# A decoder trunk of two layers: the low parts of the MLP weights of groups 1 to 7 made on VectorE from a second rounded copy that ScalarE writes into two PSUM banks

## The chip, the cores and the metric

The kernel runs on one core of a Trainium2 chip. The metric is the device time of one execution in microseconds (us). The kernel before takes 1218.79 us, the median of three runs (1218.43 to 1220.8).

## The reference

The trunk has two layers on 512 tokens of width 1024. The first mixes tokens by attention, the second by a short convolution; each is followed by an MLP of width 4096 with a squared ReLU and by a gated input embedding. All arithmetic is in float32. The part that matters here:

```python
def sq_relu_mlp(h, w_up, w_down):
    return jnp.square(jax.nn.relu(h @ w_up)) @ w_down
...
        f = sq_relu_mlp(rmsnorm(x, g[2]), w_mlp_up[i], w_mlp_down[i])
        x = x + rmsnorm(f, g[3])
        gate = jax.nn.sigmoid(rmsnorm(x, g[4]) @ w_ple_gate[i])
        e = (p[i] @ w_ple_proj[i]) * gate
        x = x + rmsnorm(e, g[5])
```

## The kernel before, in words

**High and low parts.** Every matrix product runs as three products of rounded operands (`mm3`, L268 to L270): high by high, low by high and high by low, added up in one PSUM bank. An operand x is split (`split`, L274): ScalarE writes the high part `hi`, which is x rounded to the type fp32r (L276), and another engine writes the low part, x less `hi` (L277). For a weight these tiles are called `wh` and `wl`. The other engine is VectorE, except for a few forms for which `prepare` (L175) names GpSimd: the weight sums T1 to T4 of the MLP's groups 1 to 6, and the sums S3 and S4 of the convolution's projections.

**Weights.** A fixed list (`plan` and what calls it) holds all weight tiles of 128x512 in the order of their use. SyncE's queue loads them as `raw` tiles. `prepare` walks the list some eight tiles ahead of the matmuls; for each tile it loads, and splits.

**The MLP** (`mlp`, L957) has eight groups of 512 hidden units, `gr` 0 to 7, in each layer. Groups 0 to 6 run like this:

- *Up.* For four blocks f of 128 hidden units, 8 x 3 matmuls of 128x512 fill a bank `up_<gr>_<f>`. ScalarE applies ReLU (tile `r`, L975) and squares (tile `q`, L961). Group 0 runs in two halves of 256 tokens (`r_0_2_256` is the second half of block 2); the others run whole. That is 96 matmuls of 128x512.
- The squares are cut into quarters A11 to A22, and GpSimd makes sums S1 to S4 of them (L989). Each is split into high and low parts (`A12h`, `S1h`, `S3l`); two of them share a tile.
- *Down* (`down`). The product of 2x2 blocks is done with seven products rather than eight, in the order 1, 2, 4, 5, 6, 7, 3. The weight blocks are B11 to B22 (`raw`) and the sums T1 to T4 (`dn_T`), which GpSimd makes at L168. Each product fills two banks (`dn_<gr>_50` and `dn_<gr>_51` for product 5) by 2 x 2 x 3 matmuls: 84 in all.
- The seven products are gathered in 14 accumulator tiles `acc` in SBUF. In group 0, ScalarE copies the banks there (L1018); from group 1 on, VectorE adds the bank to the tile (L1021). In group 1, these additions are also ordered behind the low part of S3 and S4 by a dependence written by hand.

Group 7 runs up like the others, and down as a plain product with eight weight tiles. Then the norm, the residual and the gated embedding follow, token tile by token tile.

**PSUM.** All eight banks come from one pool (`bank`, L83). A tile takes the bank that came free first and waits for its last reader. The names above without their numbers are those of the profile: `dn`, `up`, `acc`.

**Order.** A scheduler sets the order of the instructions on each engine when the kernel is built, so a change in `split` can move other instructions too. Each engine works through its own queue in order.

Of the kernel before, what the change touches and what calls it, by code (L numbers as in the profile page):

```python
# [9 lines left out]
F32R = mybir.dt.float32r  # L10
AF = mybir.ActivationFunctionType
ALU = mybir.AluOpType
# [42 lines left out]
ON_POOL = ('S3', 'S4')  # L55
# [13 lines left out]
def trunk(ctx: ExitStack, tc, x, xT, pT, g, gT, wv, wqk, bf, wo, wci, wcq, cw, wco, wup, wdn, wpp, wpg, out):  # L69
    nc = tc.nc  # L70
# [9 lines left out]
    def page(name, dtype=F32):  # L80
        return pages.tile([P, S], dtype, tag="pg", name=name)

    def bank(name):  # L83
        return psum.tile([P, S], F32, tag="ps", name=name)
# [67 lines left out]
    def fetch(upto):  # L152
        while len(fetched) < min(upto, len(loads)):
            n = len(fetched)
            raw = raws.tile([P, S], F32, tag="raw", name=f"raw{n}")
            fetched.append(raw)
            src = loads[n]
            nc.sync.dma_start(raw[:, : src.shape[-1]], src)

    def derive(key):  # L160
        at, sums = recipes.pop(key)
        fetch(max(at.values()) + 1)
        B = {name: fetched[n][:, :S] for name, n in at.items()}
        for name, a, b, op in sums:
            t = page("_".join(str(u) for u in (*key, *name)))
            derived[(*key, *name)] = t
            B[name] = t[:, :S]
            ins = nc.gpsimd.tensor_tensor(out=B[name], in0=B[a], in1=B[b], op=op)  # L168
            if last_norm:
                tc.add_manual_dep(  # L170
                    ins.ins, last_norm.pop().ins.name,
                    mybir.DependencyInfo(mybir.DependencyClass.Sync, mybir.DependencyReason.DATA),
                )

    def prepare(upto, lows=None):  # L175
        while begun[0] < min(upto, len(order)):
            n = begun[0]
            begun[0] += 1
            key, at = order[n]
            for of in (key[:3], key[:2]):  # L180
                if of in recipes:
                    derive(of)
            hi, lo = page(f"wh{n}", F32R), page(f"wl{n}", F32R)
            if isinstance(at, tuple):
                raw, w = derived.pop(key), S
                eng = nc.gpsimd if (key[0] == "dn" and key[2] > 0) or key[-1] in ON_POOL else nc.vector
            else:
                fetch(at + 1)
                raw, eng, w = fetched[at], lows or nc.vector, loads[at].shape[-1]
                fetched[at] = None  # L190
            if key[0] in ("v", "qk"):
                split_gained(hi, lo, raw, w, key[2], eng, key[0] == "qk" or key[1] == 2)
            else:
                split(hi[:, :w], lo[:, :w], raw[:, :w], eng)
            ready[key] = Pair(hi[:, :w], lo[:, :w])

    def wide(*key, soon=SOON):

        prepare(where[key] + 1 + soon)
        return ready[key]  # L200
# [73 lines left out]
    def split(hi, lo, src, eng=nc.vector):  # L274

        nc.scalar.copy(hi, src)  # L276
        return eng.tensor_tensor(out=lo, in0=src, in1=hi.bitcast(F32), op=ALU.subtract)  # L277

    def split_gained(hi, lo, src, w, at, eng, paired):

        parts = [(slice(0, w), at)]
        if paired:
            parts = [(slice(256 * i, 256 * i + 256), 2 * at + i) for i in range(2)]
        for c, k in parts:
            nc.scalar.mul(hi[:, c], src[:, c], first_g[:, k : k + 1])
        for c, k in parts:
            eng.scalar_tensor_tensor(
                out=lo[:, c], in0=src[:, c], scalar=first_g[:, k : k + 1],
                in1=hi[:, c].bitcast(F32), op0=ALU.mult, op1=ALU.subtract,
            )  # L290
# [49 lines left out]
    def keep(t, n, ps, hT):  # L340
        to = lambda h: h[:, 4 * n : 4 * n + 4, t * P : (t + 1) * P]
        split(to(hT.hi), to(hT.lo), ps.rearrange("p (j c) -> p j c", j=4))
# [51 lines left out]
    def mixer_out(kind, lhs, xs, gB, then, opened):  # L394


        mgs, sums = {}, {}
        for t, n in BLOCKS:
            if (t, n) == (2, 0):
                prepare(where[kind, 1, KT - 1] + 1 + SOON)  # L400
            at = (t, n) in opened
            ps = opened.pop((t, n)) if at else bank(f"{kind}{n}_{t}")
            for k in range(KT - 1 if at else 0, KT):
                mm3(ps, lhs(k, t), wide(kind, n, k, soon=soon(t, n)), k == 0, k == KT - 1)
            sums[t, n] = squares(ps, f"{kind}s{n}_{t}")
            mgs[t, n] = gained(ps, gB, n, f"{kind}m{n}_{t}")
            if (t, 1 - n) in mgs:
                residual(t, *([d.pop((t, i)) for i in range(2)] for d in (mgs, sums)), xs[t],
                         f"{kind}r")
                then(t)  # L410

    def attention(hT, raw_x, b_f, warm, work, by_hand):
# [6 lines left out]
        def logs():  # L419

            e, u, lg = stat("f_e", n_f), stat("f_u", n_f), stat("f_l", n_f)
            neg = stat("f_n", n_f)
            nc.vector.tensor_scalar(out=neg, in0=logit, scalar1=-1.0, scalar2=None, op0=ALU.mult)
            nc.vector.tensor_tensor(out=neg, in0=logit, in1=neg, op=ALU.min)
            nc.scalar.activation(e, neg, AF.Exp)
            yield
            nc.vector.tensor_scalar(out=u, in0=e, scalar1=1.0, scalar2=None, op0=ALU.add)
            nc.scalar.activation(lg, u, AF.Ln)
            rest, ru = stat("f_r", n_f), stat("f_ru", n_f)
            nc.vector.scalar_tensor_tensor(  # L430
                out=rest, in0=u, scalar=-1.0, in1=e, op0=ALU.add, op1=ALU.subtract
            )
            nc.vector.reciprocal(ru, u)
            nc.vector.tensor_tensor(out=rest, in0=rest, in1=ru, op=ALU.mult)
            yield
            nc.vector.tensor_tensor(out=lg, in0=lg, in1=rest, op=ALU.subtract)
            logf = stat("logf", n_f)
            nc.vector.scalar_tensor_tensor(
                out=logf, in0=logit, scalar=0.0, in1=lg, op0=ALU.min, op1=ALU.subtract
            )  # L440
            split(lf.hi, lf.lo, logf)
            yield
# [235 lines left out]
        def stream():  # L678
            for i in range(1, KT):
                for n, _ in enumerate(project(i)):  # L680
                    yield
                    if i == KT - 1 and n > KT:
                        streaming.clear()
                        reach[0] = (n - KT - 1) // 2
                        split_o()
            yield from out_part((0,), range(6))
            yield from out_part((1,), range(6))
            prepare(where["o", 1, KT - 1] + 1)
            yield from out_part((0, 1), (6,))
# [630 lines left out]
```

## Time and profile before

| | |
|---|---|
| median of 3 runs | 1218.79 us (1218.43 to 1220.8) |
| the profiled execution: span | 1216.5 us |
| the profiled execution: what lies around its span, taken as median less span | 2.3 us |
| mean clock granted to TensorE | 0.999 |
| TensorE (PE) | 1205.5 us busy, 6175 instructions |
| VectorE (DVE) | 931.4 us busy, 1474 instructions |
| ScalarE (ACT) | 691.4 us busy, 1465 instructions |
| GpSimd (POOL) | 655.4 us busy, 616 instructions |
| moved by DMA | 150.84 MB, mean 124 GB/s |

The profile is of one execution. Its rows name the engine, the line (L276 is line 276 of the kernel before), the operation, and the tiles as out<-in, without their numbers. A row of a time line holds the start, the duration (from the first start to the last end, if several are gathered, with their number behind x), and in brackets the idle time ahead of it with what ended it. Matmuls overlap: a row of 0.39 us may start 0.23 us behind the one ahead of it, so times are read from start to start. Casts of ScalarE overlap too, by about a tenth of a microsecond.

### The profile page before, as it was taken

Reading aid. Unit: us, or ns where it says so; the run is one execution under the profiler, and the core shown is the slowest. Engines: PE = TensorE matmul, PEld = TensorE weight load, DVE = VectorE, ACT = ScalarE, POOL = GpSimd, SP = SyncE. Lnnn points to the kernel's source line nnn. Section 1 sums busy time; section 2 is a strip of 40 time slices with the busy share of each in tenths; the row PEclk is TensorE's granted clock in tenths of the full one; section 3 lists DMA queues with packets and bytes.
Section 4 is the critical chain, followed back from the end, with each engine's and each line's share of the span. In section 5 each row is a group of like instructions: output and inputs, shape, how many; then the busy total and the mean of one; then the engine's idle time right before and its main releaser. Section 6 shows DMA issues by size and latency. Waiting matters only on the chain.

```text
span 1216.5 us, 18743 instructions
## 1 busy us (share of the span) xinstructions
PE 1205.5 (99%) x6175; PEld 1027.5 (84%) x6175; DVE 931.4 (77%) x1474; ACT 691.4 (57%) x1465; POOL 655.4 (54%) x616
## 2 busy tenths in 40 slices
PE   9999999999999999999999999999999999999997
PEld 8888887898888888888889999989888888888886
DVE  7888889586669766879877888866876787669873
ACT  7687778458644564455665534545746445645551
POOL 2035666155787877774213455126676878678210
PEclk9999999999999999999999999999999999999999
DMA  9376544623234323438223123542422443135401
GB/s 333 122 210 172 167 152 125 222 93 94 77 113 138 102 66 110 139 97 276 83 88 108 35 80 103 176 154 71 139 87 65 127 138 106 61 112 185 162 13 58
DMA packets 87314, 150.84 MB, mean 124 GB/s; under 512 B 10352, under 2 KB 18080, under 8 KB 87216
## 3 DMA queue, kind: packets, MB, share of 16 engines
q1 hardware_dynamic: 86640, 149.11, 39.3%
q8 instruction: 49, 0.80, 0.3%
q10 hardware_dynamic: 576, 0.53, 0.1%
q14 instruction: 49, 0.40, 0.1%
HBM read 139.03 MB, written 6.37 MB: 120 GB/s over the span
## 4 chain that ended last, share of the span: by engine, by line
PE 91%; ACT 3%; issue 2%; DVE 2%; POOL 1%; DMA 0%; SPq 0%; POOLq 0%; DVEq 0%; ACTq 0%
PE up L269 9%; PE up L270 9%; PE up L268 9%; PE dn L268 8%; PE dn L270 8%; PE dn L269 8%; PE v L476 3%; PE pg L269 2%; PE pg L268 2%; PE pg L270 2%; PE qk L270 2%; PE qk L269 2%; PE qk L268 2%; PE pT L590 1%; PE co L269 1%
## 5 line engine op out<-in xcount | busy, mean ns | idle before, releaser
L277 DVE TENSOR_TENSOR wl<-raw,wh 128x512 fp32r<-128x512 f32 x346 | 344.7, 1041 | 14.1 <-ACT wh L276 13.4
L269 PE MATMUL up<-hTh,wl 128*128 128x512 f32 (+1 forms) x576 | 210.2, 365 | 0.0
L270 PE MATMUL up<-hTl,wh 128*128 128x512 f32 (+1 forms) x576 | 209.6, 365 | 0.0
L268 PE MATMUL up<-hTh,wh 128*128 128x512 f32 (+1 forms) x576 | 208.7, 366 | 0.0
L276 ACT CAST wh<-raw 128x512 fp32r<-128x512 f32 x346 | 189.4, 625 | 4.5 <-DVE xd L373 4.4
L975 ACT ACTIVATE r<-up 128x512 f32<-128x512 f32 (+1 forms) x72 | 39.5, 548 | 201.8 <-PE up L270 190.1
L277 POOL TENSOR_TENSOR wl<-dn_T,wh 128x512 fp32r<-128x512 f32 x96 | 132.7, 1416 | 30.0 <-ACT wh L276 30.0
L168 POOL TENSOR_TENSOR dn_T<-raw,raw 128x512 f32<-128x512 f32 x56 | 87.0, 1564 | 69.1 <-DMA raw<-in_wdn 50.5
L269 PEld LDWEIGHTS up<-hTh,wl 128*128 128x128 f32 x576 | 108.6, 189 | 17.5
L268 PEld LDWEIGHTS up<-hTh,wh 128*128 128x128 f32 x576 | 108.6, 189 | 17.5
L270 PEld LDWEIGHTS up<-hTl,wh 128*128 128x128 f32 x576 | 108.2, 189 | 17.4
L1021 DVE TENSOR_TENSOR acc<-dn,acc 128x512 f32<-128x512 f32 x168 | 107.4, 680 | 13.9 <-PE dn L270 13.9
L168 POOL TENSOR_TENSOR dn_T<-raw,dn_T 128x512 f32<-128x512 f32 x56 | 92.5, 1651 | 2.2
L276 ACT CAST wh<-dn_T 128x512 fp32r<-128x512 f32 x112 | 61.4, 616 | 10.9 <-POOL dn_T L168 10.9
L277 DVE TENSOR_TENSOR A12l<-q,A12h 128x512 fp32r<-128x512 f32 x28 | 23.2, 829 | 53.8 <-ACT A12h L276 53.8
L1035 POOL TENSOR_TENSOR acc<-acc,acc 128x512 f32<-128x512 f32 x28 | 46.9, 1707 | 9.9 <-DVE acc L1021 9.9
L277 DVE TENSOR_TENSOR A11l<-q,A11h 128x256 fp32r<-128x256 f32 x28 | 23.2, 828 | 36.5 <-ACT A11h L276 36.5
L270 PE MATMUL qk<-hTl,wh 128*128 128x512 f32 x128 | 50.7, 396 | 0.0
L269 PE MATMUL pg<-wh,hTl 128*128 128x512 f32 x128 | 50.5, 394 | 0.0
L268 PE MATMUL pg<-wh,hTh 128*128 128x512 f32 x128 | 50.4, 394 | 0.0
L268 PE MATMUL qk<-hTh,wh 128*128 128x512 f32 x128 | 50.3, 393 | 0.0
L269 PE MATMUL qk<-hTh,wl 128*128 128x512 f32 x128 | 50.2, 392 | 0.0
(404 smaller groups left out, 3304.5 us busy)
## 6 DMA issues: line engine op xcount, KB each, us to landing
raw<-in_wup SPq DMA_DIRECT2D x128, 256.0 KB, 2.9
raw<-in_wdn SPq DMA_DIRECT2D x128, 256.0 KB, 2.8
raw<-in_wcq SPq DMA_DIRECT2D x36, 256.0 KB, 2.8
raw<-in_wqk SPq DMA_DIRECT2D x32, 256.0 KB, 5.3
raw<-in_wpg SPq DMA_DIRECT2D x32, 256.0 KB, 4.1
g<-in_g SPq DMA_DIRECT2D x22, 256.0 KB, 5.9
prl<-neg_c SPq DMA_DIRECT2D x16, 256.0 KB, 6.3
raw<-in_wo SPq DMA_DIRECT2D x16, 256.0 KB, 4.7
```

The source lines that it names most:

```text
L168: ins = nc.gpsimd.tensor_tensor(out=B[name], in0=B[a], in1=B[b], op=op)
L268: nc.tensor.matmul(ps, a.hi, b.hi, start=start, stop=False)
L269: nc.tensor.matmul(ps, a.lo, b.hi, start=False, stop=False)
L270: nc.tensor.matmul(ps, a.hi, b.lo, start=False, stop=stop)
L276: nc.scalar.copy(hi, src)
L277: return eng.tensor_tensor(out=lo, in0=src, in1=hi.bitcast(F32), op=ALU.subtract)
L476: nc.tensor.matmul(ps[:, : V_CHUNKS[c][1]], getattr(of_x(k, t), p), getattr(ready["v", c, k], of), start=k == 0 and p == of, stop=k == KT ...
L590: nc.tensor.transpose(ps[:, b * P : (b + 1) * P], probs[h][b][:, j * P : (j + 1) * P], ident)
L975: nc.scalar.activation(r[:, :n], ps[:, :n], AF.Relu)
L1021: ins = nc.vector.tensor_tensor(out=a, in0=banks[s], in1=a, op=ALU.add)
L1035: nc.gpsimd.tensor_tensor(out=a, in0=a, in1=acc[i, s][:, :S], op=ALU.add)
```

## The change

For the weights of the MLP's groups 1 to 7, up and down, `prepare` now calls a new function, `split_beside`. ScalarE rounds each weight twice: once into `hi`, as before, and once into a bank of PSUM. VectorE makes the low part from the source and the copy in PSUM, not from `hi`; the value is the same. There are two such banks for each layer, `beside_0` and `beside_1`. They are used in turn, are taken from the pool at the first use (which falls in group 0, since weights are prepared ahead), and are held until the last weight of group 7. Matmuls have six banks meanwhile. GpSimd makes no low part of T1 to T4 any more. In numbers, for both layers: 2 x (56 + 84 + 8) = 296 more casts on ScalarE; 96 low parts go from GpSimd to VectorE; loads and matmuls are the same.

```diff
             if isinstance(at, tuple):
                 raw, w = derived.pop(key), S
-                eng = nc.gpsimd if (key[0] == "dn" and key[2] > 0) or key[-1] in ON_POOL else nc.vector
+                eng = nc.gpsimd if key[-1] in ON_POOL else nc.vector
...
             if key[0] in ("v", "qk"):
                 split_gained(hi, lo, raw, w, key[2], eng, key[0] == "qk" or key[1] == 2)
+            elif key[0] in ("up", "dn") and key[2] > (key[0] == "up"):
+                split_beside(hi[:, :w], lo[:, :w], raw[:, :w], key[1])
             else:
                 split(hi[:, :w], lo[:, :w], raw[:, :w], eng)
...
+    besides = {}
+
+    def split_beside(hi, lo, src, l):
+
+        n = besides[l, "n"] = 1 - besides.get((l, "n"), 1)
+        if (l, n) not in besides:
+            besides[l, n] = bank(f"beside{l}_{n}")
+        again = besides[l, n][:, : src.shape[-1]]
+        nc.scalar.copy(again.bitcast(F32R), src)
+        nc.scalar.copy(hi, src)
+        nc.vector.tensor_tensor(out=lo, in0=src, in1=again, op=ALU.subtract)
```

(The third number of an "up" key counts half groups, so the condition holds from group 1 on for both.)

The two places at which the new order matters most lie in the down step of group 0. The first is on ScalarE, from the last half block of up to the accumulator copies. Before (line, operation, out<-in; L975 is ReLU, L961 the square, L276 a cast to a high part, L1018 a copy of a bank to an accumulator):

```order
L975 ACTIVATE r_0_2_256_4063<-up_0_2_256_4038 128x256
L961 ACTIVATE q_0_2_3750<-r_0_2_256_4063 128x256
L975 ACTIVATE r_0_3_256_4093<-up_0_3_256_4068 128x256
L961 ACTIVATE q_0_3_3751<-r_0_3_256_4093 128x256
L276 CAST A12h_0_3_4096<-q_0_3_3751 128x512
...
L1018 COPY acc_1_0_4134<-dn_0_10_4112 128x512
L1018 COPY acc_1_1_4136<-dn_0_11_4113 128x512
L276 CAST wh_4140<-dn_0_T_0_3771 128x512
L276 CAST wh_4150<-dn_0_T_1_3779 128x512
L1018 COPY acc_2_0_4160<-dn_0_20_4138 128x512
L1018 COPY acc_2_1_4162<-dn_0_21_4139 128x512
```

And of the changed kernel, whose lines lie up to 14 lower in the file:

```order
L989 ACTIVATE r_0_2_256_4063<-up_0_2_256_4038 128x256
L975 ACTIVATE q_0_2_3750<-r_0_2_256_4063 128x256
L289 CAST beside_0_4196<-raw_4194 128x512
L989 ACTIVATE r_0_3_256_4093<-up_0_3_256_4068 128x256
L975 ACTIVATE q_0_3_3751<-r_0_3_256_4093 128x256
...
L1032 COPY acc_1_0_4134<-dn_0_10_4112 128x512
L1032 COPY acc_1_1_4136<-dn_0_11_4113 128x512
L278 CAST wh_4140<-dn_0_T_0_3771 128x512
L289 CAST beside_1_4210<-raw_4208 128x512
L278 CAST wh_4150<-dn_0_T_1_3779 128x512
L1032 COPY acc_2_0_4160<-dn_0_20_4138 128x512
L1032 COPY acc_2_1_4162<-dn_0_21_4139 128x512
```

The first two weights of group 1 get their copies here: one cast moves in ahead of the last ReLU of group 0, and one between the casts of two weights of product 6 and 7, ahead of the copies of product 2. Layer 1 has the same order.

The second place is on TensorE, in the same step (product 5, around the second half of products 2 and 4). Before:

```order
L268 MATMUL dn_0_50_4190<-wh_3881,S1h_0_1_4030 128x512
L269 MATMUL dn_0_50_4190<-wh_3881,S1l_0_1_4031 128x512
L270 MATMUL dn_0_50_4190<-wl_3882,S1h_0_1_4030 128x512
L268 MATMUL dn_0_51_4191<-wh_3881,S1h_0_1_4030 128x512
L269 MATMUL dn_0_51_4191<-wh_3881,S1l_0_1_4031 128x512
L270 MATMUL dn_0_51_4191<-wl_3882,S1h_0_1_4030 128x512
L268 MATMUL dn_0_20_4138<-wh_3815,A12h_0_3_4096 128x512
...
L268 MATMUL dn_0_50_4190<-wh_3891,S1h_0_3_4104 128x512
L268 MATMUL dn_0_51_4191<-wh_3891,S1h_0_3_4104 128x512
```

And of the changed kernel:

```order
L270 MATMUL dn_0_50_4190<-wh_3881,S1h_0_1_4030 128x512
L271 MATMUL dn_0_50_4190<-wh_3881,S1l_0_1_4031 128x512
L272 MATMUL dn_0_50_4190<-wl_3882,S1h_0_1_4030 128x512
L270 MATMUL dn_0_20_4138<-wh_3815,A12h_0_3_4096 128x512
...
L272 MATMUL dn_0_50_4190<-wl_3892,S1h_0_3_4104 128x512
L270 MATMUL dn_0_51_4191<-wh_3881,S1h_0_1_4030 128x512
L271 MATMUL dn_0_51_4191<-wh_3881,S1l_0_1_4031 128x512
L272 MATMUL dn_0_51_4191<-wl_3882,S1h_0_1_4030 128x512
L270 MATMUL dn_0_51_4191<-wh_3891,S1h_0_3_4104 128x512
```

The second bank of product 5 is filled as a whole behind the first. With two banks fewer, other tiles share banks: `dn_0_50` takes the bank that the last ReLU (`r_0_3_256`) empties, before that of `r_0_2_256`; `dn_0_51` that which the first copy of product 1 empties (`acc_1_0`); and `dn_0_60`, product 6, that of `dn_0_20`, which `acc_2_0` empties, where before it took that of `dn_0_10`, which `acc_1_0` empties.

## The prediction

> **What bounds the kernel now.** I read the page first, then the chain of waits, the windows and the time lines of single engines around the MLP. The page's busy times and the chain's engine line (share of the span by engine):
>
> ```profile
> PE 1205.5 (99%) x6175; PEld 1027.5 (84%) x6175; DVE 931.4 (77%) x1474; ACT 691.4 (57%) x1465; POOL 655.4 (54%) x616
> PE 91%; ACT 3%; issue 2%; DVE 2%; POOL 1%; DMA 0%; SPq 0%; POOLq 0%; DVEq 0%; ACTq 0%
> ```
>
> TensorE bounds the kernel, and only some 11 us of the 1216.5 are not its own. Rows of the chain that start two groups in the MLP of each layer (start, duration, engine, tile, line), and the window of one group (columns: PE, PEld, DVE, ACT, POOL busy, then clock, DMA share, GB/s):
>
> ```profile
> 322.03 0.45 PE dn L268 x2
> 362.83 0.45 PE dn L268 x2
> 932.80 0.91 PE dn L268 x4
> 973.60 0.91 PE dn L268 x4
> ...
> 363.00:404.00 41.00, 41.00 (x183) 33.96 (x182) 31.82 (x37) 20.55 (x38) 31.15 (x24) 1.00 0.32 103
> ```
>
> Both pairs lie exactly 40.80 us apart. A group has 96 + 84 = 180 matmuls, so each takes 0.2267 us and nothing is lost between them. In groups 1 to 6 the low parts are hidden, whoever makes them. A gain for VectorE or GpSimd there has no stall to remove; ScalarE, 20.55 us of 41, has room. What can change the time is a place where the new casts or the two missing banks reach TensorE. The tightest is the down step of group 0, where ScalarE empties the banks. TensorE's rows there (layer 0):
>
> ```profile
> 280.59 0.39 PE L270 MATMUL dn<-wl,A12h 128*128 128x512 f32 x1
> 280.89 0.50 PE L268 MATMUL dn<-wh,S1h 128*128 128x512 f32 x1
> ...
> 282.18 0.40 PE L270 MATMUL dn<-wl,S1h 128*128 128x512 f32 x1
> 282.71 1.20 PE L268 MATMUL dn<-wh,A12h 128*128 128x512 f32 x4
> 283.75 0.39 PE L269 MATMUL dn<-wh,A12l 128*128 128x512 f32 x1
> ...
> 286.71 0.39 PE L270 MATMUL dn<-wl,S1h 128*128 128x512 f32 x1
> 287.03 0.50 PE L268 MATMUL dn<-wh,S1h 128*128 128x512 f32 x1
> ```
>
> The last row is product 6 (dn_0_60). ScalarE's rows of the same time:
>
> ```profile
> 281.19 0.37 ACT L975 ACTIVATE r<-up 128x256 f32<-128x256 f32 x1
> ...
> 282.04 0.62 ACT L276 CAST A12h<-q 128x512 fp32r<-128x512 f32 x1
> ...
> 285.36 1.14 ACT L276 CAST wh<-dn_T 128x512 fp32r<-128x512 f32 x2
> 286.40 1.06 ACT L1018 COPY acc<-dn 128x512 f32<-128x512 f32 x2
> 287.36 1.15 ACT L276 CAST wh<-dn_T 128x512 fp32r<-128x512 f32 x2
> 288.40 1.08 ACT L1018 COPY acc<-dn 128x512 f32<-128x512 f32 x2
> ```
>
> From 285.36 ScalarE never pauses: two casts of weights, two copies of accumulators, and again. Product 6 starts at 287.03, right behind the first copy of 286.40 (x2 in 1.06 us, the first done near 286.98): TensorE already waits on ScalarE here for a bank.
>
> **The change, part by part.** First the prices: casts of ScalarE in one unbroken row, the same cast by itself and at half width, the two kinds of low part, the accumulator's addition (which reads a bank of PSUM), and a low part while GpSimd is idle (groups: total busy us, mean ns of one, then the idle time before them):
>
> ```profile
> 364.81 7.39 ACT L276 CAST wh<-raw 128x512 fp32r<-128x512 f32 x14
> ...
> L276 ACT CAST wh<-raw 128x512 fp32r<-128x512 f32 x346 | 189.4, 625 | 4.5 <-DVE xd L373 4.4
> L276 ACT CAST A11h<-q 128x256 fp32r<-128x256 f32 x28 | 11.4, 407 | 0.9
> ...
> L277 DVE TENSOR_TENSOR wl<-raw,wh 128x512 fp32r<-128x512 f32 x346 | 344.7, 1041 | 14.1 <-ACT wh L276 13.4
> L277 POOL TENSOR_TENSOR wl<-dn_T,wh 128x512 fp32r<-128x512 f32 x96 | 132.7, 1416 | 30.0 <-ACT wh L276 30.0
> L1021 DVE TENSOR_TENSOR acc<-dn,acc 128x512 f32<-128x512 f32 x168 | 107.4, 680 | 13.9 <-PE dn L270 13.9
> 393.48 0.69 DVE L277 TENSOR_TENSOR S1l<-s,S1h 128x512 fp32r<-128x512 f32 x1 [2.10 <-ACT S1h L276]
> ```
>
> *One more cast, b.* Fourteen casts in 7.39 us are one every 0.52 us (7.39 less the last one's 0.62, by 13). No row shows ScalarE writing to PSUM. From below I bound b by the half-width cast's 0.41 less the 0.09 by which neighbours overlap (0.62 - 0.52): 0.32; from above by the lone cast's 0.625. I take 0.52, since these casts stand in a queue and have the same shape. The Trainium skill (ScalarE: Activation LUTs, section "Step-by-step: what each stage is for") says that ScalarE writes to PSUM faster than to SBUF, but that this only pays where TensorE doesn't need most of PSUM. By its first half b would lie below 0.52, and with the lower bound the sum below is 5.3 instead of 6.1 us; its second half speaks against this change, and the waits for a bank at 287.03 agree with it.
>
> *A low part on VectorE.* 1.04 us now, mean; 0.69 undisturbed; 0.68 for the addition with a bank as one operand, while GpSimd works. I take 0.68 for the new form, as the nearest row. A group has 8 + 14 = 22 of these low parts, 14 on VectorE and 8 on GpSimd before. VectorE: 31.82 - 14 x 1.04 + 22 x 0.68 = 32.2 us of 40.8 (at 1.04 it would be 40.1). GpSimd: 31.15 - 8 x 1.42 = 19.8. ScalarE: 20.55 + 22 x 0.52 = 32.0. All fit, so groups 2 to 6 cost and gain nothing: the cover is 40.8 us of matmuls, the fullest engine under it 32.2. The Trainium skill (Advanced Engine Details and Errata, section "GPSIMD Details") has GpSimd share a read and a write interface with VectorE, with conflicts where VectorE reads two operands of SBUF. The rows (1.04 with two, 0.68 with a bank) agree; without this rule VectorE would stand at 40.1 of 40.8, a rival below.
>
> *Group 0's down step.* The order of the changed kernel puts the first cast into a bank between q_0_2 and the last relu (281.19), the second between the two weight casts of 287.36. Both stand ahead of accumulator copy 2. And with two banks gone, product 6 no longer takes the bank of product 1 but that of product 2; it waits for the copy of 288.40 rather than that of 286.40. So:
> - the copy comes 288.40 - 286.40 = 2.00 us later in the queue;
> - two casts ahead of it: 2 x 0.52 = 1.04 us;
> - product 6 at 287.03 + 3.04 = 290.07.
>
> On the way TensorE stands in pieces that add up to this, not on top of it: product 5's first bank now waits for the relu (done at 281.56 before, 282.08 now, against 280.89); A12h comes 0.52 later; product 5's second bank waits for acc 1's copy (287.5). TensorE is bound and wins none of it back: from there on its next banks (products 7, 3, group 1's up) are copied 0.6 us or more ahead of it. The low parts and weights aren't late, as the raw weight of the first cast landed long before. Layer 1 has the same order:
>
> ```profile
> 854.98 0.50 PE L268 MATMUL dn<-wh,S1h 128*128 128x512 f32 x1
> 854.36 1.06 ACT L1018 COPY acc<-dn 128x512 f32<-128x512 f32 x2
> 856.35 1.08 ACT L1018 COPY acc<-dn 128x512 f32<-128x512 f32 x2
> ```
>
> There 856.35 - 854.36 + 1.04 = 3.03 us.
>
> *Group 1.* Between accumulator copy 2 and S3h of group 1's last pair ScalarE gets 16 more casts, with the two before them 18 x 0.52 = 9.4 us. Its pauses there (in brackets):
>
> ```profile
> 303.03 0.60 ACT L975 ACTIVATE r<-up 128x512 f32<-128x512 f32 x1 [1.40 <-PE up L270]
> 306.43 0.60 ACT L975 ACTIVATE r<-up 128x512 f32<-128x512 f32 x1 [1.70 <-PE up L270]
> 311.33 0.62 ACT L276 CAST S1h<-s 128x512 fp32r<-128x512 f32 x1 [2.98 <-POOL s L989]
> ...
> 317.31 0.60 ACT L975 ACTIVATE r<-up 128x512 f32<-128x512 f32 x1 [0.86 <-PE up L270]
> ...
> 321.17 0.62 ACT L276 CAST S1h<-s 128x512 fp32r<-128x512 f32 x1 [1.95 <-POOL s L989]
> ```
>
> They hold 8.9 us, and TensorE itself comes 3 us later, so this just fits. But VectorE's accumulator additions of group 1 stand behind S3's low part by a dependence written by hand, and banks wait for them. I take 0 and keep 1 us a layer (two casts) for the range.
>
> *Group 7, and what follows the MLP*: the same casts in place of none, eight weights that lie ready early; taken at nothing, the cover being the group's 96 + 192 matmuls.
>
> The sum: 3.04 + 3.03 = 6.07, or 6.1 us. The profiled execution goes from 1216.5 to 1222.6 us of span. The median stands 2.3 us above the span (1218.79 against 1216.5: what lies around it), so the time is 1218.8 + 6.1 = **1224.9 us**, 0.5% slower. A measurement here can tell 0.2%, 2.4 us, from no change.
>
> **The rivals.**
> *A, the forecast*: chance 0.80.
> *B, ScalarE becomes the bound in every group.* Its pauses for GpSimd's sums stay, in a group:
>
> ```profile
> 392.83 0.62 ACT L276 CAST S1h<-s 128x512 fp32r<-128x512 f32 x1 [2.88 <-POOL s L989]
> ...
> 402.67 0.62 ACT L276 CAST S1h<-s 128x512 fp32r<-128x512 f32 x1 [1.84 <-POOL s L989]
> ```
>
> With these 4.7 us its group is 20.55 + 4.7 + 22b; it passes 40.8 at b = 0.71. At 0.8, 42.9: 2.1 us x 12 groups = 25 us, and group 0's 2 x 3.6 = 7.2: 1251 us. For it: no row shows the cast. Against: every cast in the trace is below 0.63, and GpSimd, relieved, ends those pauses earlier. Chance 0.06.
> *C, no change, by relief.* VectorE's low parts drop to 0.68, and TensorE's waits in the MLP go: in the rows above 0.07 us before 280.89, 0.30 before 282.71, 0.13 before 283.75, 0.09 before 287.03, 0.6 a layer, 1.2 in all: 1217.6. It decides if product 6 doesn't wait for copy 2, if ScalarE, say, ran its queue with 3 us to spare there. Against: it shows no pause from 285.36 on, and a start of TensorE right behind a copy. Chance 0.09.
> *D, VectorE becomes the bound.* The low part stays at 1.04: 40.1 us, and the pause of 2.10 at 393.48 makes 42.2: 1.4 x 12 = 17 us, with the 6.1 of group 0 1242 us. Against: 168 additions at 0.68. Chance 0.05.
>
> **How the numbers follow.** Low end: b = 0.32 gives 2 x (2.00 + 0.64) = 5.3; less 1.2 of relief, less the 0.4 by which the fastest run lies under the median: 1222.5. High end: b = 0.625 gives 6.5, two stalls of 1 us in group 1, and the 2.0 us by which the slowest run lies above the median: 1229.3. B, C and D, 0.20 together, stay outside. Slower: A, B, D less a little of A's low end, 0.89. Same: C, 0.09 with that little. Faster, for which no row has 2.4 us to give: 0.02.
>
> **What would show it.** In the profile of the changed kernel: product 6 of group 0 near 290.1 in layer 0, with TensorE's pauses before it on ScalarE's relu, A12h and copies; the starts of groups from there on 40.80 us apart; ScalarE's casts into banks at 0.5 to 0.6 us; VectorE's low parts at 0.68; GpSimd some 11 us less busy a group. It is wrong if groups are over 40.8 us apart (B or D by the engine that is full), or if product 6 starts within a microsecond of 287.03 (C).

## The result, and the profile after

The changed kernel takes 1236.06 us (median of 4 runs, 1235.27 to 1236.92) against 1219.0 us of the kernel before on the same chip. The ratio is 1.0138, with a 95% interval of 1.0124 to 1.0153: slower by 17.1 us. The forecast was 1224.9 us, with a range up to 1229.3; the sign was right, and about a third of the loss was in the sum.

The page's busy times, and the engine line of the chain of waits, of the changed kernel:

```profile
PE 1211.1 (98%) x6175; PEld 1028.2 (83%) x6175; DVE 869.3 (70%) x1570; ACT 851.5 (69%) x1761; POOL 475.6 (39%) x520
PE 84%; ACT 5%; DVE 4%; issue 4%; POOL 3%; DMA 1%; SPq 0%; POOLq 0%; DVEq 0%; ACTq 0%
```

VectorE and GpSimd have less to do, ScalarE 160 us more, about as forecast (296 casts at 0.52 us are 154). In the chain TensorE's share fell from 91% to 84%: another 7% of the span now hang on other engines. Not in the groups, though. The chain's rows at the start of group after group, and the window of one group (columns as before: PE, PEld, DVE, ACT, POOL busy, clock, DMA share, GB/s):

```profile
326.75 0.91 PE dn L270 x4
367.55 0.91 PE dn L270 x4
408.35 0.91 PE dn L270 x4
...
367.55:408.35 40.80, 40.80 (x181) 33.78 (x181) 27.29 (x45) 32.98 (x61) 16.78 (x16) 1.00 0.34 103
```

They are 40.80 us apart as before, with ScalarE at 33.0 us (forecast 32.0), VectorE at 27.3 (32.2) and GpSimd at 16.8 (19.8). The view of waits says where TensorE now stands (us in all, how often, the longest):

```profile
PE dn L270 <- ACT acc L1032: 3.0, 4, 0.9
PE pg L271 <- DVE hTl L279: 2.0, 2, 1.8
PE dn L270 <- ACT r L989: 2.0, 2, 1.3
...
PE c L271 <- DVE wl L279: 1.3, 2, 1.1
...
PE pg L270 <- ACT hTh L278: 0.9, 2, 0.6
PE n0b_p L351 <- DVE n0b_h L342: 0.6, 1, 0.6
PE pg L272 <- DVE wl L279: 0.5, 1, 0.5
```

The rows of `dn` are group 0's. Those of `pg` (the embedding's gate), `n0b_p` and `c` (the start of the convolution) lie behind the MLP, and the kernel before has hardly any of them. To put a size on each place, take the start of the same matmul in both traces. Before:

```profile
250.56 0.28 PE L268 MATMUL up<-hTh,wh 128*128 128x256 f32 x1
583.67 0.39 PE L268 MATMUL pp<-wh,wh 128*128 128x512 f32 x1
643.67 0.28 PE L268 MATMUL c<-hTh,wh 128*128 128x256 f32 x1
819.02 0.28 PE L268 MATMUL up<-hTh,wh 128*128 128x256 f32 x1
1151.60 0.39 PE L268 MATMUL pp<-wh,wh 128*128 128x512 f32 x1
```

And after:

```profile
251.20 0.28 PE L270 MATMUL up<-hTh,wh 128*128 128x256 f32 x1
587.71 0.39 PE L270 MATMUL pp<-wh,wh 128*128 128x512 f32 x1
650.54 0.28 PE L270 MATMUL c<-hTh,wh 128*128 128x256 f32 x1
829.62 0.28 PE L270 MATMUL up<-hTh,wh 128*128 128x256 f32 x1
1165.27 0.39 PE L270 MATMUL pp<-wh,wh 128*128 128x512 f32 x1
```

The delays are 0.64, 4.04, 6.87, 10.60 and 13.67 us, and 16.75 at the last matmul (1209.71 and 1226.46). So each MLP costs 3.4 and 3.1 us, the embedding stage of layer 0 another 2.8, the convolution 3.7 and the embedding stage of layer 1 3.1. (The first 0.64 lies ahead of the change; this stage differs by 0.2 to 1.5 us between profiled executions of kernels that are alike there.)

Not all of the convolution's 3.7 us is waiting. Right behind the wait at `c`, the clock granted to TensorE was 0.50 for 3.4 us (two windows of the changed kernel, columns as before):

```profile
663.60:667.00 3.40, 3.21 (x15) 2.91 (x15) 3.40 (x5) 3.40 (x10) 3.40 (x3) 0.50 0.49 144
667.00:670.40 3.40, 3.40 (x30) 3.40 (x30) 3.40 (x6) 3.40 (x10) 0.84 (x1) 1.00 0.51 153
```

Both windows hold matmuls of 128x256, 15 in the first and 30 in the second, so this slow stretch cost some 1.7 us (an estimate from these two rows); the waits make up the rest. Runs 1, 2 and 4 below have one such stretch each behind group 7 of layer 0 (3.4, 3.4 and 6.8 us), run 7 has six, and the kernel before and the other runs have none but in the last 5 us. Each begins in a wait of TensorE or within 2 us of the end of one, but not every wait has one: the 1.8 us at `pg`, which ends at 603.07 of the changed kernel, has none. Which waits bring it stays open.

The group 0 part is the one that was forecast. ScalarE, layer 0, after:

```profile
282.20 0.58 ACT L289 CAST beside<-raw 128x512 fp32r<-128x512 f32 x1
282.71 0.37 ACT L989 ACTIVATE r<-up 128x256 f32<-128x256 f32 x1
...
287.93 1.06 ACT L1032 COPY acc<-dn 128x512 f32<-128x512 f32 x2
...
289.40 0.60 ACT L289 CAST beside<-raw 128x512 fp32r<-128x512 f32 x1
289.92 0.62 ACT L278 CAST wh<-dn_T 128x512 fp32r<-128x512 f32 x1
290.44 1.08 ACT L1032 COPY acc<-dn 128x512 f32<-128x512 f32 x2
```

And TensorE at the same place:

```profile
283.14 0.50 PE L270 MATMUL dn<-wh,S1h 128*128 128x512 f32 x1 [1.30 <-ACT r L989]
...
288.55 0.50 PE L270 MATMUL dn<-wh,S1h 128*128 128x512 f32 x1 [0.61 <-ACT acc L1032]
...
291.09 0.50 PE L270 MATMUL dn<-wh,S1h 128*128 128x512 f32 x1 [0.88 <-ACT acc L1032]
```

The second bank of product 5 waits for accumulator copy 1, product 6 (291.09) for copy 2. A cast into a bank holds the queue for 0.51 or 0.52 us (282.20 to 282.71, 289.40 to 289.92).

### The profile page after: what moved, and what is told of

It is laid out like the page before. It is cut to its first block, busy times and chain, and to the rows that moved or that the text cites. A ratio compares the mean times of both kernels' runs of the same rounds, so it can differ in the third digit from the quotient of the medians.

```text
span 1233.7 us, 18895 instructions
## 1 busy us (share of the span) xinstructions
PE 1211.1 (98%) x6175; PEld 1028.2 (83%) x6175; DVE 869.3 (70%) x1570; ACT 851.5 (69%) x1761; POOL 475.6 (39%) x520
## 4 chain that ended last, share of the span: by engine, by line
PE 84%; ACT 5%; DVE 4%; issue 4%; POOL 3%; DMA 1%; SPq 0%; POOLq 0%; DVEq 0%; ACTq 0%
PE up L272 9%; PE up L270 9%; PE up L271 9%; PE dn L270 8%; PE dn L272 7%; PE dn L271 7%; PE v L490 2%; PE qk L272 2%; PE qk L271 2%; PE qk L270 2%; ACT junk L326 1%; PE pT L604 1%; PE o L272 1%; PE co L270 1%; PE co L271 1%
## 5 line engine op out<-in xcount | busy, mean ns | idle before, releaser
L291 DVE TENSOR_TENSOR wl<-raw,beside 128x512 fp32r<-128x512 f32 x200 | 129.0, 682 | 38.7 <-ACT beside L289 37.8
L289 ACT CAST beside<-raw 128x512 fp32r<-128x512 f32 x200 | 116.2, 596 | 31.0 <-DVE wl L291 27.2
L168 POOL TENSOR_TENSOR dn_T<-raw,raw 128x512 f32<-128x512 f32 x56 | 73.8, 1331 | 161.5 <-PE dn L272 60.5
L279 DVE TENSOR_TENSOR wl<-raw,wh 128x512 fp32r<-128x512 f32 x146 | 114.5, 825 | 14.6 <-ACT wh L278 11.7
L290 ACT CAST wh<-raw 128x512 fp32r<-128x512 f32 x200 | 117.9, 626 | 0.0
L278 ACT CAST wh<-raw 128x512 fp32r<-128x512 f32 x146 | 82.4, 623 | 5.4 <-PE dn L272 3.4
L168 POOL TENSOR_TENSOR dn_T<-raw,dn_T 128x512 f32<-128x512 f32 x56 | 74.4, 1329 | 2.2
L289 ACT CAST beside<-dn_T 128x512 fp32r<-128x512 f32 x96 | 54.2, 587 | 15.3 <-DVE wl L291 12.4
L291 DVE TENSOR_TENSOR wl<-dn_T,beside 128x512 fp32r<-128x512 f32 x96 | 61.7, 681 | 1.9 <-ACT beside L289 1.9
L1003 POOL TENSOR_TENSOR s<-q 128x256 f32<-128x256 f32 x28 | 20.7, 740 | 105.2 <-ACT q L975 105.2
L290 ACT CAST wh<-dn_T 128x512 fp32r<-128x512 f32 x96 | 54.7, 617 | 0.0
```

The costliest lines, as they stand in the source:

```text
L289: nc.scalar.copy(again.bitcast(F32R), src)
L291: nc.vector.tensor_tensor(out=lo, in0=src, in1=again, op=ALU.subtract)
L1003: sums = lambda out, a, b, op: nc.gpsimd.tensor_tensor(out=out, in0=a, in1=b, op=op)
```

## The experiments

All runs are of one core, as the kernel before. Behind each median stand, in brackets, its ratio to the kernel before on the same chip (medians there 1218.99 to 1219.31 us) and the 95% interval of the ratio. The table at the end of this section gives TensorE's delay by stage for all of them. The changed kernel's down step of group 7 was the first suspect. Its 96 matmuls serve four token tiles of 24 each, and the program order of the two kernels differs there: tile 0 is done after 45 matmuls before, and after 58 in layer 0 and 64 in layer 1 of the changed kernel. Behind it come tile 0's norm, and behind that the embedding stage. VectorE's first four additions of that work (one row holds them), of before and then of after:

```profile
571.86 2.48 DVE L1078 TENSOR_TENSOR acc<-dn,acc 128x512 f32<-128x512 f32 x4 [1.85 <-PE dn L270]
```

```profile
578.84 2.48 DVE L1092 TENSOR_TENSOR acc<-dn,acc 128x512 f32<-128x512 f32 x4 [5.90 <-PE dn L272]
```

They are 6.98 us apart, 2.94 more than TensorE's own delay of 4.04 at that time: 13 matmuls of 0.2267 us. From there on the chain of the changed kernel no longer runs over TensorE but over the norms, an engine at a time:

```profile
584.41 0.67 DVE xd L387
585.16 0.74 ACT junk L326 x2
586.38 0.57 POOL n_r_y L321
...
587.64 0.75 DVE n_h L342
...
590.20 1.34 DVE xd L387 x2
```

**1. The changed kernel with group 7's matmuls in the old order.** A list holds the order of the 96 matmuls, each ordered behind the last by a dependence without a wait:

```diff
-        for t in range(NB):
-            ...
-                mm3(banks[n], tokens_of(hs[f], t), w, f == 0, f == 3)
+        for code in SEVENTH[l].split():
+            t, n, f, p = (int(c) for c in code)
+            ...
+            ins = nc.tensor.matmul(banks[t][n], a.lo if p == 1 else a.hi, w.lo if p == 2 else w.hi, ...)
+            if prev is not None:
+                tc.add_manual_dep(ins.ins, prev.ins.name, NoSync)
```

> The changed kernel, with the 96 matmuls of each layer's group 7 down step held in the order that the kernel before has there (by scheduling dependences from one matmul to the next, no waits). Theory (order): of the 17 us lost, some 10 come from this order alone: tiles 0 and 1 end 13 matmuls (2.9 us) later in layer 0 and 19 (4.3 us) later in layer 1, and the norms and the gated embedding behind them follow. Then about 1225.5 to 1226.5 us. Rival (load): the embedding stage is late because ScalarE and VectorE are late with group 7's casts and low parts, or for want of banks; then it stays near 1236 us.

1234.92 us (ratio 1.0134, 1.0119 to 1.0149): the theory failed here, or was too narrow, and the number is close to the rival's. VectorE in that run shows what else had moved:

```profile
575.56 0.69 DVE L1113 TENSOR_TENSOR acc<-dn,acc 128x512 f32<-128x512 f32 x1 [5.37 <-PE dn L1096]
576.16 0.68 DVE L283 TENSOR_TENSOR wl<-raw,wh 128x512 fp32r<-128x512 f32 x1
...
582.17 1.40 DVE L391 SCALAR_TENSOR_TENSOR xd<-acc,mr_r_y,xd 128x512 f32<-128x512 f32 x2
```

And the first residual of the kernel before:

```profile
575.49 0.74 DVE L373 SCALAR_TENSOR_TENSOR xd<-acc,mr_r_y,xd 128x512 f32<-128x512 f32 x1
```

Tile 0's sums come 3.7 us behind those of before, as TensorE does. But the residual `xd` comes at 582.17, where before it began at 575.49: 6.7 us. Low parts of the embedding's weights now stand between the sums. Only the 96 matmuls were held; the scheduler, which orders each engine when the kernel is built, had set VectorE's and ScalarE's order anew as well, and TensorE's behind the 96.

**2. The kernel before with group 7's matmuls in the new order.** The same edit on the kernel before. Its order behind group 7 in layer 0 then equals that of the changed kernel on all four engines, while no cast, low part or bank is added or taken away.

> The kernel before, with nothing changed but the order of the matmuls of group 7's down step, held in the order of the changed kernel. Theory (order): about +10 us, 1228 to 1230 us, with the same stalls behind group 7 as in the changed kernel. Rival (load): within 1 us of 1219.

1228.98 us (1.0082, 1.0067 to 1.0097), 9.9 us lost, with the waits of the changed kernel behind group 7 and none in group 0:

```profile
PE pg L273 <- DVE hTl L281: 3.8, 2, 2.0
PE c L273 <- DVE wl L281: 1.8, 2, 1.1
```

So an order alone, with the work of the kernel before, is enough for the whole loss behind group 7 (10.2 us in the table, 9.6 in the changed kernel). In layer 0 that is more than the 2.9 us by which tile 0 ends later: the order on VectorE and ScalarE moved with it, and the slow stretch of the clock falls in the embedding stage here.

**3. Two banks held, no casts.**

```diff
...
+            if key in FIRST_TWO:
+                l, n = FIRST_TWO[key]
+                held[l, n] = bank(f"held{l}_{n}")
+                nc.scalar.copy(held[l, n][:, :1], raw[:, :1])
+            if key in LAST_TWO:
+                l, n = LAST_TWO[key]
+                nc.vector.tensor_tensor(out=junk[:, :1], in0=raw[:, :1], in1=held[l, n][:, :1], op=ALU.subtract)
```

> The kernel before, with two PSUM banks taken at the first two weights of group 1 (a ScalarE copy of one column into each) and held to the last two weights of group 7 (a VectorE subtraction of one column), and no other cast: the loss of banks alone. Group 7's down order is that of before. Theory (the bank of product 6 is copied out two copies and two casts later): 2.0 us a layer for the bank and 0.2 a layer for each one-column copy, in all 4.4 to 5 us: about 1223.5 to 1224; nothing lost behind group 7. Rival 1 (the casts, not the banks, cost in group 0): 1219 to 1219.8. Rival 2 (want of banks also delays the stage behind group 7): about 1233.

1226.61 us (1.0058, 1.0041 to 1.0075), 3 us more than the theory's figure. Waits of TensorE:

```profile
PE dn L279 <- ACT acc L1029: 2.1, 4, 0.6
PE up L279 <- DVE acc L1032: 2.0, 3, 0.7
```

Group 0 lost about 2.3 us a layer, as forecast for the banks with two copies of one column; nothing was lost behind group 7. The difference is the row of `up`: three starts of a group waited for VectorE's accumulator additions to free a bank (0.84 us from start to start each, 2.5 in all). The changed kernel, with six banks too and a VectorE that has less to do, has no such row. So the relief of VectorE seems to have a worth there, but only against the loss of banks; no run relieves VectorE alone.

**4. The copies for groups 2 to 6 alone, group 7's matmuls in the old order.** The condition becomes 3 < key[2] < 14 for up and 1 < key[2] < 7 for down.

> The changed kernel with the second copy used only for the weights of groups 2 to 6 (groups 1 and 7 are split as before, on VectorE and GpSimd), and group 7's down step held in the order of before. Theory: the stall in group 0 and those behind group 7 are gone and the groups between cost and gain nothing: within 1 us of 1219. Rival (ScalarE or VectorE lose time in the groups between): slower by over 2 us with starts of groups over 40.80 us apart. Rival (relief pays): faster by over 1 us.

1224.61 us (1.0043, 1.0028 to 1.0058). The MLPs lost nothing (0.02 and -0.05 us in the table). But the theory's number failed again behind group 7: 1.2 us in the embedding stage and 5.3 in the convolution's start, none in layer 1. Here too only the order of group 7's 96 matmuls was held. Of the 5.3 us, some 3.4 (estimated as above) are the slow stretch of 6.8 us, which begins at 658.18 in the convolution's first matmuls.

**5. The changed kernel with the order of three engines held behind group 7.** Every instruction of TensorE, VectorE and ScalarE from group 7's down step to the next MLP (in layer 1 to the end) is put behind its predecessor in the order of before:

```diff
+    for names in FOLLOW:
+        names = [f"I-{n}" for n in names.split()]
+        for first, second in zip(names, names[1:]):
+            tc.add_manual_dep(made[second], first, NoSync)
```

> The changed kernel, with the order of TensorE, VectorE and ScalarE held, from the start of group 7's down step to the next MLP (and to the end in layer 1), in the order that the kernel before has there; nothing else is altered. The run with TensorE's order alone held left 1234.9 us, and in it VectorE and ScalarE had weight splits of the embedding stage between the first accumulator additions and the norm. Theory (order of all three engines): the stalls behind group 7 go, the 6.1 to 6.3 us of group 0 stay: 1225 to 1226 us. Rival (load: ScalarE and VectorE really are late there with group 7's casts, or banks are short): 1230 us or more, with TensorE waiting at the same places.

1228.85 us (1.0079, 1.0064 to 1.0094): by the table, 6.4 of the 9.6 us behind group 7 came back and 3.3 stayed. This lies between the two theories.

**6. The same order, copies for groups 2 to 7.** No cast and no loss of a bank in group 0 (key[2] > 3 for up, > 1 for down).

> The second copy only for the weights of groups 2 to 7 (group 1's are split as before, so no copy is written and no bank taken in group 0), and the order behind group 7 held as before. Theory (the loss is group 0's queue on ScalarE plus the order behind group 7, nothing else): 1218.5 to 1220 us, the time of before. Rival (the copies cost time in the groups between, or in group 7): over 1221 us. Rival (relief of VectorE and GpSimd pays): under 1217.5 us.

1222.87 us (1.0031, 1.0019 to 1.0042): group 0's part is gone, as the theory has it, but the 3.3 us behind group 7 are there again, so the number is that of the first rival. ScalarE at that place, of before and then of this run:

```profile
576.26 0.62 ACT L276 CAST wh<-raw 128x512 fp32r<-128x512 f32 x1 [2.20 <-DVE xd L373]
576.78 0.63 ACT L312 ACTIVATE junk<-xd 128x512 f32<-128x512 f32 x1
```

```profile
579.05 0.62 ACT L74 CAST wh<-raw 128x512 fp32r<-128x512 f32 x1 [4.82 <-PE dn L74]
579.58 0.63 ACT L74 ACTIVATE junk<-xd 128x512 f32<-128x512 f32 x1
```

Same order, but the cast of one weight of the embedding's gate waits 2.6 us longer (0.17 of the 2.79 is the delay of the run): no longer for VectorE, but for TensorE's last reading of a weight of group 7. So this tile seems to get another page of SBUF from the pool, one freed later; that is read from the wait alone. Behind the cast, in ScalarE's queue, stand the squares of tile 0's residual, on which the norm waits.

**7. The casts into SBUF.** `again` becomes one of two fixed SBUF tiles; the page pool is two pages smaller; the order behind group 7 is held.

> The changed kernel with the second copy written into two fixed SBUF tiles instead of PSUM banks (two pages fewer in the page pool), and the order behind group 7 held as before: all the casts and VectorE's low parts, with no bank lost. In group 0 no cast stands ahead of the accumulator copies of products 1 and 2 here. Theory (group 0's loss is the banks and the two casts ahead of the copies): group 0 costs under 1 us, in all 1219 to 1221 us, unless VectorE's low parts, with two operands of SBUF, stay near 1.0 us and fill VectorE (40 of 40.8 us a group by my sum): then groups over 40.80 us apart and up to 1242 us. Rival (the casts themselves cost in group 0): about 1225 us.

1281.68 us (1.051, 1.0494 to 1.0526), worse than any theory's number. Two groups of low parts of this run, from loaded weights and from sums, and then the first of them in the changed kernel:

```profile
L74 DVE TENSOR_TENSOR wl<-raw,beside 128x512 fp32r<-128x512 f32 x200 | 234.9, 1228 | 9.0 <-ACT beside L74 8.0
L74 DVE TENSOR_TENSOR wl<-dn_T,beside 128x512 fp32r<-128x512 f32 x96 | 63.4, 698 | 2.2 <-ACT beside L74 2.2
```

```profile
L291 DVE TENSOR_TENSOR wl<-raw,beside 128x512 fp32r<-128x512 f32 x200 | 129.0, 682 | 38.7 <-ACT beside L289 37.8
```

With two operands in SBUF the 200 low parts of loaded weights take 1.23 us, mean, the 96 of sums 0.70 (the last section says what tells them apart); with one operand in a bank all take 0.68. ScalarE waits for VectorE to free the two tiles (85.5 us in all), and all that stands behind a cast comes late: groups last up to 43.3 us, 43.10 in this window:

```profile
456.90:500.00 43.10, 42.07 (x181) 33.26 (x181) 34.64 (x45) 33.37 (x61) 19.43 (x17) 1.00 0.32 98
```

VectorE is busy for 34.6 of the 43.1 us. So it isn't full, as the theory's second number had it; in its place the trace shows ScalarE waiting for a free tile, and TensorE waiting for ScalarE's high part `A11h` at the start of a down step (9.6 us in 10 waits). The embedding and convolution stages lost 23 us too, in spite of the held order. TensorE also ran at a granted clock of 0.50 for 23.9 us in six stretches, by estimate some 12 us of the whole loss. How much of all this the smaller page pool adds was not tried. The run's own question has an answer all the same: TensorE's waits for group 0's accumulator copies, 3.0 us in the changed kernel, are gone, with no bank lost and no cast ahead of those copies.

**8. The kernel before, group 7 tile by tile.** The list of run 2 in plain order, 24 matmuls for each tile in turn.

> The kernel before, with group 7's down step in plain order, tile by tile: tile 0 ends after 24 matmuls rather than 45, 4.8 us earlier. Theory (the norms behind group 7 set TensorE's waits only when they come late): the kernel before loses some 1 us behind group 7, so at best 1 us is won, 1218 us, if ScalarE and VectorE keep the order of the norms; TensorE may stall up to 1 us at the last hidden block in group 7. Rival (each matmul by which tile 0 ends earlier is worth as much as each by which it ended later, about 0.3 us for one in each layer): 1212 to 1214 us.

1219.93 us (1.0005, 0.9995 to 1.0015): no change that can be told. To end tile 0 earlier than before is worth nothing. There was little to win: the longest wait of TensorE behind group 7 of the kernel before is the 0.3 us at `c`. And VectorE's order moved here too: tile 0's sums began 4.5 us earlier, but its residual only 1.8 us earlier, and its norm (`n_h`) 1.8 us later.

**9 and 10. One cast moved.** In runs 5 and 6 the cast that waits for its page goes behind the two squares, and its low part behind the next addition.

> The changed kernel with the order behind group 7 held as before, except for one weight of the embedding stage in each layer (the second of the gate's): its cast on ScalarE stands behind the two squares of tile 0's residual instead of ahead of them, and its low part on VectorE one instruction later. In the run with the whole old order (1228.9 us), this cast waits for a page of SBUF until TensorE has read group 7's weights, and the squares behind it came 2.6 us late. Theory (this wait, at the head of ScalarE's queue, is what was left behind group 7): the norm of tile 0 is late by some 1.3 us (low part and tile 1's squares still wait) instead of 2.6, TensorE's stall of 1.7 us a layer behind group 7 falls to about 0.5: 1226 to 1227 us. Rival (the chain is late for another reason): 1228.5 to 1229.5, no change.

> The same move in the kernel that uses the second copy for groups 2 to 7 with the old order behind group 7 (1222.9 us without the move). Theory: 1220 to 1221 us. Rival (the copies of group 7, or the groups between, cost what is left): 1222.5 to 1223.5 us.

1225.08 us (1.0047, 1.0031 to 1.0064) and 1219.63 us (0.9999, 0.999 to 1.0008), 0.9 and 0.4 us below the theory's lowest figures. TensorE's waits behind group 7 are gone. In the first of the two, the longest rows left in the MLP and behind it are

```profile
PE dn L74 <- ACT acc L74: 3.0, 4, 0.9
PE dn L74 <- ACT r L74: 1.8, 2, 1.1
...
PE c L74 <- DVE wl L74: 0.4, 1, 0.4
```

which is group 0's loss, and the 0.3 that the kernel before has at `c`. The second has the copies of groups 2 to 7 and the time of before. So neither the casts nor the two banks cost anything behind group 7 once the order, that cast included, is as in these two runs.

TensorE's delay against before, in us, by the starts of the same matmuls as above and of the last one; each column but the last holds what was added from one of them to the next:

| kernel | ahead of the MLP | MLP 0 | embedding 0 | convolution | MLP 1 | embedding 1 | at the last matmul |
|---|---|---|---|---|---|---|---|
| changed | 0.64 | 3.40 | 2.82 | 3.74 | 3.07 | 3.08 | 16.75 |
| 1 changed, old order of group 7's matmuls | 0.64 | 3.06 | 2.31 | 4.43 | 2.99 | 2.24 | 15.67 |
| 2 before, new order | 1.36 | 0.12 | 4.40 | 2.86 | -0.03 | 2.99 | 11.70 |
| 3 banks held | 1.22 | 4.07 | 0.00 | 0.00 | 3.09 | 0.00 | 8.38 |
| 4 groups 2 to 6 | 0.50 | 0.02 | 1.18 | 5.25 | -0.05 | 0.03 | 6.93 |
| 5 changed, old order of three engines | 1.16 | 3.08 | 1.66 | -0.04 | 3.00 | 1.63 | 10.49 |
| 6 groups 2 to 7, same | 0.20 | -0.03 | 1.71 | -0.02 | 0.28 | 1.62 | 3.76 |
| 7 casts into SBUF, same | 1.16 | 21.56 | 8.21 | 6.47 | 18.03 | 8.28 | 63.71 |
| 8 before, tile by tile | 0.48 | -0.01 | -0.03 | 0.51 | 0.03 | -0.05 | 0.93 |
| 9 as 5, one cast moved | 0.82 | 3.00 | 0.00 | 0.10 | 3.00 | 0.00 | 6.92 |
| 10 as 6, one cast moved | 1.45 | -0.03 | 0.00 | -0.03 | -0.03 | 0.00 | 1.36 |

## Why the prediction was wrong

**Right: the bound and the groups between.** TensorE bounds both kernels. Groups 2 to 6 cost and gain nothing (runs 4 and 10), and no other engine became full; rivals B and D fell, with casts at 0.52 us in the queue and low parts at 0.68. The relief of rival C is worth nothing by itself (run 10 has it in groups 2 to 7). Two readings against the rivals were a little off: single casts of the kernel before last up to 0.73 us, not 0.63, and the low part at 393.48 still meets GpSimd in its first 0.13 us. Neither changed a term.

**Right: group 0, mechanism and size.** Product 6 was put at 3.04 and 3.03 us late. The runs with casts in group 0 show 3.0 to 3.1 a layer, the changed kernel's own profile 3.40 in layer 0. Banks alone cost about 2.3 with their one-column copies, the forecast being 2.0 and the copies. Runs 9 and 10, which differ by group 0 and group 1, stand 5.5 us apart: the forecast was 6.1. Group 1's 0 to 1 us was taken at 0, and no wait shows there.

**Wrong: one step.** It reads: "*Group 7, and what follows the MLP*: the same casts in place of none, eight weights that lie ready early; taken at nothing, the cover being the group's 96 + 192 matmuls." That stretch cost 2.82 + 3.74 + 3.08 = 9.6 us. The cover is real for TensorE's total, and TensorE doesn't stall in group 7. What the total leaves out is the order behind it. That order was set anew, and the chain of norms that follows, which passes through ScalarE, GpSimd and VectorE in turn, has about 1 us of slack against TensorE (run 6: 2.6 us late costs 1.7). In the changed kernel tile 0 ended 13 and 19 matmuls later, but that is only one part: in run 1 it ended as before, and 9.0 us were lost all the same. Runs 1, 2, 5, 6, 9 and 10 show three ways in which the chain was late: TensorE's order (never without the second), the order of weight splits among the sums on VectorE and ScalarE, and a cast at the head of ScalarE's queue that waits for an SBUF page freed late. With all three undone (run 9), the changed kernel loses only group 0's part. Of the 9.6 us, some 1.7 are TensorE at half clock behind the wait at `c`, which the sum didn't have either. The high end of the range, 1229.3, held stalls in group 1, but none behind group 7. The change was said to have the two places at which the order matters most in group 0's down step; the matmuls of group 7 are a third, which cost more, and their order could have been read in the same way.

What stays open: what TensorE's new order costs by itself, since no run has it without a new order of VectorE and ScalarE; and why the order was set as it was. That the scheduler's own model of ScalarE's load moved it is a guess; no run tests that.

## What to carry to other kernels

Where a scheduler orders the instructions when the kernel is built, a change also reorders stages that it doesn't touch, so compare the whole order, and ask for each bound engine not only how much it does but which consumer's last input moved. Find the chains that have little slack against the bound engine, norms and other serial steps at a change of stage, and price whatever comes to stand ahead of them in a queue. And look for what stands at the head of an in-order queue with a wait on a buffer: its cost is that of all that stands behind it.

## What the runs showed of the hardware that was not expected

A subtraction of two 128x512 operands on VectorE took 0.68 us with one operand in PSUM, whatever GpSimd did: of the changed kernel's 200 low parts of loaded weights, 107 lie wholly under GpSimd's work, and their mean is 0.68 too. With both operands in SBUF (run 7) it depends on GpSimd. Of the 200 there, the 65 that meet no work of GpSimd took 0.68 us, and the 92 that lie wholly under it 1.67 us, mean, and up to 1.82. The 96 of sums, of which 94 meet none, took 0.70. The Trainium skill (Advanced Engine Details and Errata, section "GPSIMD Details") names the shared interface on which such instructions conflict with GpSimd's. These rows agree, and give the size: 1.0 us, mean, on a low part that meets GpSimd all along. A cast of ScalarE into PSUM took 596 ns against 626 into SBUF, mean of 200 each, but both hold the queue for 0.52 us. The Trainium skill (ScalarE: Activation LUTs, section "Step-by-step: what each stage is for") has PSUM as the faster target: the trace shows 0.03 us in the length of one and nothing in the queue, and agrees that it only pays where TensorE can spare the banks: two banks alone cost about 2.3 us a layer in group 0 (run 3).
